# Attention scores over 256 keys in place of 210, 146 and 82

## The chip, the core and the metric

The kernel runs on one core of a Trainium2 chip. Its time is the device time of one execution in microseconds (us). The engines are named as in the profile: PE (TensorE's products), PEld (its weight loads), DVE (VectorE), ACT (ScalarE), POOL (GpSimd) and SP (SyncE, which issues most transfers). A line such as L606 is a line of the kernel before; the program of the changed kernel counts one line more from L467 on and two more from L598 on.

## The reference

One block of a streaming encoder on 1024 frames and 16 meta tokens, 1024 features wide: a SwiGLU half step, a mixer, a second half step, and RMS norms. The mixer adds a sliding-window attention and a gated linear attention, each behind a gate. The attention, cut to what matters here:

```python
CHUNK = 64; N_META = 16; ATT_HEADS = 8; ATT_KV_HEADS = 2; ATT_HEAD_DIM = 64
WINDOW = 128; WINDOW_CHUNKS = WINDOW // CHUNK
...
s_band = jnp.einsum('bcqkgd,bcskd->bkgcqs', qf, kb) * scale
s_band = s_band - slopes[None, :, :, None, None, None] * dist[None, None, None]
s_band = jnp.where(valid, s_band, -jnp.inf)
s_meta = jnp.einsum('bcqkgd,bmkd->bkgcqm', qf, km) * scale
p = jax.nn.softmax(jnp.concatenate([s_meta, s_band, s_sink], axis=-1), axis=-1)
of = (einsum(p[meta], vm) + einsum(p[band], vb))
```

So each chunk of 64 queries sees its own 64 keys, the 128 before them, the 16 meta keys and one learned sink per head. All of it is in 32-bit floating point.

## The kernel before

Features lie on partitions, tokens along the free dimension. To keep 32-bit precision, both operands of a product are split in two halves of type fp32r, and a product is three (L88 to L90): high by high, high by low, low by high. Weights are streamed in tiles of 128x1024 and split by ACT (L196, the high half) and DVE (L197, the low half).

The mixer goes through the keys' and values' projections, those of the queries, the attention, its branch matrix, the gated linear attention, the second branch and the output matrix. The attention loop runs over 16 chunks of 64 queries, c = 0 to 15.

Keys lie in `kh` (high halves, one tile for each of the two groups of heads) and `kl` (low halves), in 8 blocks of 146 columns: 16 meta keys, a column for the sink, a pad, and 128 frames (two chunks). A chunk's keys are one stretch of columns from `off`, `w` wide: 82 columns for c = 0, 146 for c = 1, and 210 for the other 14, which start either behind a block's meta keys or in the middle of its frames. `qs` holds the queries of a group: their high halves on the 64 partitions of the group's own head dimension, their low halves on the other 64.

`scores(c)` makes four products of a pair of halves, two for each group of heads: L606 takes all 128 rows of the queries against `kh`, which holds the high halves of the keys twice, and L607 the 64 rows of the high halves against `kl`. A bank of PSUM (512 columns) holds the two results of a group, 256 columns each. L610 adds the bias on DVE and takes the maximum of each row, L613 scales it, L615 is the exponential on ACT, L616 the reciprocal of the sums and L618 the normalisation, in four instructions, one for each pair of heads.

`turn` transposes the probabilities (L633, PE), by two kinds of key block (82, 128 or, for the second chunk, 18 keys), and splits them (L93 on ACT, L94 on DVE). `attend` multiplies them with the values (L649): eight products of 256 columns, or four for the first chunk, which has one kind of block. L655 to L660 put the result in the queries' place. `values` turns two chunks of values every second iteration (L566 to L570 on PE, L579 and L580 on ACT, L581 on DVE).

In each iteration of the loop, one unit of another projection stands between scores and attend: the fill, 24 products of 512 columns of the attention's gate (tile `pj`), which DVE evacuates at L455 (tile `g`) before it is stored.

```python
    for c in range(16):
        nxt = None
        turn(cur)
        if c < 15:
            nxt = scores(c + 1)
        if c % 2 == 0 and c < 14:
            values(c // 2 + 1)
        if fill:
            fill.pop(0)()
        attend(cur)
        cur = nxt
```

A scheduler of the language puts the instructions of each engine in an order of its own, by costs that it reckons for them. An engine works through its order as it stands, and waits at an instruction whose input is not there.

Of the kernel before, what the change touches and what calls it, by code (L numbers as in the profile page):

```python
# [29 lines left out]
# columns of w_in  # L30
# [5 lines left out]
def hybrid_kernel(  # L36
# [32 lines left out]
    def load_vectors(vs, eng):  # L69
        """per-feature vectors, transposed to one column per tile of 128 features"""  # L70
        at, n = vs[0][0], sum(v[2] for v in vs)
        vrow = ttile("vrow")[0:32, 0:P]
        for a, v, k in vs:
            eng.dma_start(out=vrow[a - at:a - at + k, :], in_=v.rearrange("o (k p) -> (o k) p", p=P))

        def turn():
            vps = bank("vps")
            nc.tensor.transpose(vps[:, 0:n], vrow[0:n, :], ident[0:n, 0:n])
            nc.scalar.copy(vec[:, at:at + n], vps[:, 0:n])
        return turn  # L80

    def mm(ps, wh, wl, xh, xl, between=()):
        """ps = sum_k w[k].T @ x[k] with both operands split in two exact halves."""
        n = len(wh)
        for k in range(n):
            if k < len(between):
                between[k]()
            nc.tensor.matmul(ps, wh[k], xh[k], start=(k == 0), stop=False)  # L88
            nc.tensor.matmul(ps, wh[k], xl[k], start=False, stop=False)  # L89
            nc.tensor.matmul(ps, wl[k], xh[k], start=False, stop=(k == n - 1))  # L90
# [5 lines left out]
    # ------------------------------------------------------------------ rms norms  # L96
# [3 lines left out]
    class Norm:  # L100
        """Splits g*h into two halves as h is completed, tile by tile, and gathers the squares for
        the row scales 1/rms, which the consumers apply to their products."""
# [14 lines left out]
        def put(self, m, c0, n, h, copy=None):  # L117
            """h: [P, n], final"""
            g = vec[:, self.g + m:self.g + m + 1]
            hi, lo = self.hi[m][:, c0:c0 + n], self.lo[m][:, c0:c0 + n]  # L120
            nc.scalar.activation(hi, h, AF.Copy, scale=g)
            if copy is not None and m % 2:
                nc.scalar.copy(copy, h)
            nc.vector.scalar_tensor_tensor(lo, h, g, hi.bitcast(F32), op0=ALU.mult, op1=ALU.subtract)  # L124
            if copy is not None and m % 2 == 0:
                nc.vector.tensor_copy(copy, h)
# [10 lines left out]
        def total(self, c0, n):  # L137
            """sums of squares, one token to a partition"""
            ps = bank("tot")
            for t, w in tiles_of(c0, n):  # L140
                nc.tensor.matmul(ps[0:w, t:t + 1], self.acc[:, t * P:t * P + w], ones[:, 0:1], start=True, stop=True)
            self.root(c0, n, ps)

        def root(self, c0, n, tot):
            """tot: sums of squares, one token to a partition"""
            ts = tiles_of(c0, n)
            for lo, hi, w in ((ts[0][0], min(ts[-1][0] + 1, 8), P), (8, ts[-1][0] + 1, NM)):
                if lo < hi:
                    r = self.tot[0:w, lo:hi]
                    nc.scalar.activation(r, tot[0:w, lo:hi], AF.Sqrt, bias=eps_t[0:w, :], scale=1.0 / D)  # L150
                    nc.vector.reciprocal(r, r)

        def widen(self, c0, n, dg):
            """1/rms by token to rows of 128"""
            ts = tiles_of(c0, n)
            for w in (P, NM):
                mine = [t for t, v in ts if v == w]
                if mine:
                    a, k = mine[0] * P - c0, len(mine)
                    nc.vector.tensor_copy(  # L160
                        dg[0:w, a:a + k * P].rearrange("p (a b) -> p a b", b=P),
                        self.tot[0:w, mine[0]:mine[0] + k].unsqueeze(2).to_broadcast([w, k, P]))

        def spread(self, c0, n, dg=None):
            """acc becomes 1/rms on all partitions"""
            ps = bank("rep")
            if dg is None:
                dg = ttile("dg")
                self.widen(c0, n, dg)
            for t, w in tiles_of(c0, n):  # L170
                a = t * P - c0
                nc.tensor.transpose(ps[:, a:a + w], dg[0:w, a:a + P], ident[0:w, 0:w])
            nc.scalar.copy(self.acc[:, c0:c0 + n], ps[:, 0:n])  # L173

    # ------------------------------------------------------------------ weights
    class Weights:
        """streams weights in tiles of 4 KiB a partition, splitting each in its two halves"""
# [4 lines left out]
        def raw(self, views, eng=None):  # L182
            """views: (rows of the tile, columns of the tile, source)"""
            pool = self.rs[self.j % len(self.rs)]
            self.j += 1
            raw = atile("raw")[:, 0:1024] if pool is act else pool.tile([P, 1024], F32, tag="raw", name="raw")
            for rows, dst, src in views:
                (eng or nc.sync).dma_start(out=dst(raw[rows, :]), in_=src)
            return raw
# [22 lines left out]
    # ------------------------------------------------------------------ swiglu, macaron half step  # L212
    class Ffn:
# [13 lines left out]
        def gate_up(self, f, hook=None, pump=None):  # L227
            """hook: called between products; says how many chunks have their row scales"""
# [59 lines left out]
    # ------------------------------------------------------------------ load, transpose, ffn 1  # L288
# [20 lines left out]
    def warm(n):  # L309
        """products that keep the clock of the tensor engine up while it waits for input"""  # L310
# [29 lines left out]
    def pump1(i):  # L340
        """the next chunk's transposes, between the products of this one"""
# [36 lines left out]
    # the first chunk tile by tile as it comes in  # L378
# [31 lines left out]
    # ------------------------------------------------------------------ mixer  # L410
# [3 lines left out]
    def after_products():  # L414
        """work that waited for products to cover its latency"""
# [11 lines left out]
    def project_units(views, chunks, evac, m=P, k=KT, pre=None):  # L427
        """closures, one per chunk of tokens: [m features] of u @ w_in"""
# [32 lines left out]
    # ---- attention: keys and values of each pair of chunks lie as [meta, sink, pad | 128 frames]  # L461
# [4 lines left out]
    W = 3 * 64 + MB  # L466
    qs = [ap_.tile([P, 16, 256], F32R, name=f"qs{g}") for g in range(2)]  # L467
# [16 lines left out]
    def build_bias():  # L484
        """-8 slope |distance| by parity of the chunk, group of heads and pair of heads in it"""
# [75 lines left out]
    def values(j):  # L561
        """values by token: the pair, [meta | first chunk], [second chunk | next meta], each as
        [high 0 | low 0 | low 1 | high 1 | high 0 | 0 | high 1] by group"""
# [22 lines left out]
    def scores(c):  # L586
        """probabilities of chunk c's queries, rows (pair of heads' halves, 64 queries)"""
# [8 lines left out]
        s.w, s.c = w, c  # L596
        mx = sml.tile([P, 4], F32, tag="mx", name="mx")
        sm = sml.tile([P, 4], F32, tag="sm", name="sm")  # L598
        s.p = ap_.tile([P, 4, W], F32, tag="p", name="p", bufs=2)
        for g in range(2):  # L600
            own = slice(g * 64, g * 64 + 64)
            ps = bank("sp")
            for a in range(2):
                q = qs[g][:, c, a * P:(a + 1) * P]
                o = ps[:, a * 256:a * 256 + w]
                nc.tensor.matmul(o, q, kh[g][:, off:off + w], start=True, stop=False)  # L606
                nc.tensor.matmul(o, q[own], kl[own, off:off + w], start=False, stop=True)  # L607
            for a in range(2):
                ga = 2 * g + a
                nc.vector.tensor_tensor_reduce(  # L610
                    s.p[:, ga, 0:w], ps[:, a * 256:a * 256 + w], bias[:, par * 4 + ga, W - w:W], 1.0, -3.0e38,
# [9 lines left out]
    def turn(s):  # L621
        """transposes the probabilities by kind of key block, and splits them"""
# [16 lines left out]
    def attend(s):  # L639
        """rows (group, head dim), columns (head of the group, query); takes the queries' place"""  # L640
# [9 lines left out]
        # a group's rows hold high V P, the other group's rows hold its low V high P  # L650
# [30 lines left out]
    # ---- attention's branch  # L681
    class Frames:
        """columns by frame of a view by chunk and place in it"""
# [7 lines left out]
    def branch(views, y, m0, load, evac, k=4):  # L691
        """two tiles of 128 columns of a [512, 1024] branch matrix"""
# [26 lines left out]
    # ---- gated linear attention, two chunks of 64 at a time  # L719
# [7 lines left out]
    # rows of gate_w, twice for the two halves of its input's weights: [high | high | low]  # L727
# [26 lines left out]
    def ev_tok(tok, meta):  # L754
        """scales and turns a tile of 128 features to rows of tokens"""
# [17 lines left out]
    # the forget gate's low-rank input, its two halves of weights side by side  # L773
# [21 lines left out]
    class Gla:  # L795
        """two heads"""
# [13 lines left out]
        def decays(self):  # L810
# [8 lines left out]
            # 16 log_a = min(z, 0) - log(1 + exp(-|z|)), summed up within each pair of chunks  # L819
# [4 lines left out]
            # against a pair's start, middle and end  # L824
# [116 lines left out]
    # ---- merge  # L941
# [37 lines left out]
    # ------------------------------------------------------------------ ffn 2 and the last norm  # L979
# [19 lines left out]
    def tail(t, last):  # L999
        """the last norm of 128 tokens, and their store"""  # L1000
# [63 lines left out]
```

## Time and profile before

| | |
|---|---|
| median of 3 runs | 2207.11 us (2205.82 to 2207.81) |
| span of the profiled execution, first to last instruction | 2204.7 us |
| mean granted clock of PE | 0.999 |
| DVE busy, over the span | 1020.6 us (46%) |
| attention loop, first score product to its last attend | 832.6 to about 1000 us |
| transfers, mean over the span | 67 GB/s |

No time other than its span is given for the profiled execution. Matmuls are pipelined: the duration of one row overlaps that of the next, so what a product takes of PE is read from the distance between two starts. A row of PEld is the load of the weights of a product; in a steady stream it starts with the product ahead of the one it is for.

### The profile page before, as it was taken

The page shows a single profiled execution, that of the slowest core. Times are in us where ns is not written, and L with a number is a line of the kernel's source. Part 1 is how long each engine was busy: PE and PEld are TensorE (multiplying, and loading weights), DVE is VectorE, ACT ScalarE, POOL GpSimd, SP SyncE. Part 2 cuts the span into 40 slices and gives each one's busy share as a digit, 9 for nine tenths or more (in the row PEclk, how much of TensorE's full clock was granted, in tenths as well). Part 3 has the DMA queues.
Part 4 walks back from the last instruction along what each step waited for, and adds up shares of the span by engine and source line. Part 5 has one row for each costly group of instructions (what it writes and reads, how often), then busy time and mean ns, then how long its engine had stood idle before and what let it go on. Part 6 is the DMA issues. An engine that isn't in the chain of part 4 may idle for free. (4 is left out here: it accounts for less than half of the span.)

```text
span 2204.7 us, 28132 instructions
## 1 busy us (share of the span) xinstructions
PE 2193.7 (100%) x11633; PEld 1942.1 (88%) x11633; DVE 1020.6 (46%) x1781; ACT 582.6 (26%) x1068; POOL 110.6 (5%) x157
## 2 busy tenths in 40 slices
PE   9999999999999999999999999999999999999998
PEld 8999999999999997888997788888888888888888
DVE  4544544445443546663524347334444444444434
ACT  6221111211111435553323233331111111111112
POOL 1000000000000350000100000210000000000003
PEclk9999999999999999999999999999999999999999
DMA  4211111111111221116211216541111101111102
GB/s 155 67 58 39 48 49 39 58 39 58 39 39 49 90 54 44 58 53 189 58 44 63 72 56 203 164 161 48 58 48 39 57 30 57 58 48 42 55 29 77
DMA packets 178192, 148.34 MB, mean 67 GB/s; under 512 B 15494, under 2 KB 151808, under 8 KB 178064
## 3 DMA queue, kind: packets, MB, share of 16 engines
q1 hardware_dynamic: 176400, 143.81, 21.3%
q10 hardware_dynamic: 1312, 2.63, 0.3%
q8 instruction: 91, 1.49, 0.3%
q14 instruction: 37, 0.30, 0.0%
q0 software_dynamic: 352, 0.11, 0.0%
HBM read 121.36 MB, written 25.17 MB: 66 GB/s over the span
## 5 line engine op out<-in xcount | busy, mean ns | idle before, releaser
L196 ACT CAST whi<-raw 128x1024 fp32r<-128x1024 f32 x182 | 188.9, 1049 | 661.2 <-PE pd L89 370.1
L88 PE MATMUL pd<-mh,whi 128*128 128x384 f32 (+3 forms) x912 | 313.7, 344 | 0.0
L89 PE MATMUL pd<-ml,whi 128*128 128x384 f32 (+3 forms) x912 | 313.6, 344 | 0.0
L90 PE MATMUL pd<-mh,wlo 128*128 128x384 f32 (+3 forms) x912 | 313.4, 344 | 0.0
L197 DVE TENSOR_TENSOR wlo<-raw,whi 128x1024 fp32r<-128x1024 f32 x179 | 218.2, 1233 | 54.0 <-ACT whi L196 48.8
L88 PE MATMUL pj<-u2h,whi 128*128 128x512 f32 (+2 forms) x608 | 230.3, 379 | 0.0
L90 PE MATMUL pj<-u2h,wlo 128*128 128x512 f32 (+2 forms) x608 | 225.8, 371 | 0.0
L89 PE MATMUL pj<-u2l,whi 128*128 128x512 f32 (+2 forms) x608 | 225.0, 370 | 0.0
L90 PEld LDWEIGHTS pd<-mh,wlo 128*128 128x128 f32 x912 | 171.7, 188 | 14.0
L89 PEld LDWEIGHTS pd<-ml,whi 128*128 128x128 f32 x912 | 171.5, 188 | 14.1
L88 PEld LDWEIGHTS pd<-mh,whi 128*128 128x128 f32 x912 | 171.6, 188 | 14.0
L88 PE MATMUL pu<-u1h,whi 128*128 128x384 f32 (+1 forms) x528 | 171.0, 324 | 0.6 <-ACT u1q L173 0.6
L88 PE MATMUL pg<-u1h,whi 128*128 128x384 f32 (+1 forms) x528 | 169.7, 321 | 1.7 <-ACT whi L196 1.7
L89 PE MATMUL pg<-u1l,whi 128*128 128x384 f32 (+1 forms) x528 | 169.9, 322 | 0.2 <-DVE u1l L124 0.2
L244 DVE TENSOR_TENSOR a<-pu,a 128x384 f32<-128x384 f32 (+2 forms) x110 | 64.7, 588 | 225.8 <-PE pu L90 225.4
L90 PE MATMUL pg<-u1h,wlo 128*128 128x384 f32 (+1 forms) x528 | 168.5, 319 | 0.6 <-DVE wlo L197 0.6
L89 PE MATMUL pu<-u1l,whi 128*128 128x384 f32 (+1 forms) x528 | 169.2, 320 | 0.0
L90 PE MATMUL pu<-u1h,wlo 128*128 128x384 f32 (+1 forms) x528 | 168.5, 319 | 0.4 <-POOL wlo L197 0.4
L276 DVE SCALAR_TENSOR_TENSOR g<-pd,g 128x512 f32<-128x512 f32 (+1 forms) x168 | 111.9, 666 | 118.0 <-PE pd L90 117.1
L276 DVE SCALAR_TENSOR_TENSOR h<-pd,h 128x384 f32<-128x384 f32 (+1 forms) x240 | 122.8, 518 | 80.1 <-PE pd L90 79.4
L242 ACT ACTIVATE a<-a 128x384 f32<-128x384 f32 (+2 forms) x110 | 60.3, 548 | 293.9 <-DVE a L241 293.7
L88 PE MATMUL pg<-u3h,whi 128*128 128x512 f32 x352 | 137.9, 392 | 0.0
(272 smaller groups left out, 3842.2 us busy)
## 6 DMA issues: line engine op xcount, KB each, us to landing
raw<-in_ffn_w_gate SPq DMA_DIRECT2D x44, 512.0 KB, 5.0
raw<-in_ffn_w_up SPq DMA_DIRECT2D x44, 512.0 KB, 4.0
raw<-in_ffn_w_down SPq DMA_DIRECT2D x44, 512.0 KB, 3.5
raw<-in_w_in SPq DMA_DIRECT2D x30, 512.0 KB, 3.9
gates<-g SPq DMA_DIRECT2D x32, 256.0 KB, 2.0
gl<-gates SPq DMA_DIRECT2D x32, 256.0 KB, 4.2
x<-in_x SPq DMA_DIRECT2D x8, 512.0 KB, 6.6
ga<-gates SPq DMA_DIRECT2D x16, 256.0 KB, 3.5
```

The lines of the kernel that those rows point to most:

```text
L88: nc.tensor.matmul(ps, wh[k], xh[k], start=(k == 0), stop=False)
L89: nc.tensor.matmul(ps, wh[k], xl[k], start=False, stop=False)
L90: nc.tensor.matmul(ps, wl[k], xh[k], start=False, stop=(k == n - 1))
L196: nc.scalar.copy(hi[:, 0:cols], raw[:, 0:cols])
L197: (eng or nc.vector).tensor_sub(lo[:, 0:cols], raw[:, 0:cols], hi[:, 0:cols].bitcast(F32))
L242: nc.scalar.activation(a, a, AF.Silu)
L244: nc.vector.tensor_mul(a, pu[:, 0:n], a)
L276: nc.vector.scalar_tensor_tensor(hm, ps[:, 0:n], 0.5, hm, op0=ALU.mult, op1=ALU.add)
```

## The change

The score products take 256 columns of keys for every chunk. They start at `k0`, which is `off`, or, where 256 columns from there would end beyond the keys (only for c = 15, by 46 columns), the last place at which they don't. The columns that a chunk doesn't attend to are computed and not read: L610 reads the `w` columns at `off - k0` of each result.

```diff
+    SW = 256
...
         s.w, s.c = w, c
+        k0 = min(off, 8 * KB - SW)
...
             for a in range(2):
                 q = qs[g][:, c, a * P:(a + 1) * P]
-                o = ps[:, a * 256:a * 256 + w]
-                nc.tensor.matmul(o, q, kh[g][:, off:off + w], start=True, stop=False)
-                nc.tensor.matmul(o, q[own], kl[own, off:off + w], start=False, stop=True)
+                o = ps[:, a * SW:(a + 1) * SW]
+                nc.tensor.matmul(o, q, kh[g][:, k0:k0 + SW], start=True, stop=False)
+                nc.tensor.matmul(o, q[own], kl[own, k0:k0 + SW], start=False, stop=True)
             for a in range(2):
                 ga = 2 * g + a
                 nc.vector.tensor_tensor_reduce(
-                    s.p[:, ga, 0:w], ps[:, a * 256:a * 256 + w], bias[:, par * 4 + ga, W - w:W], 1.0, -3.0e38,
+                    s.p[:, ga, 0:w], ps[:, a * SW + off - k0:a * SW + off - k0 + w], bias[:, par * 4 + ga, W - w:W], 1.0, -3.0e38,
                     op0=ALU.add, op1=ALU.max, accum_out=mx[:, ga:ga + 1])
```

The rest of the diff takes out comments and docstrings. The order that the scheduler makes changes as well, on PE, DVE and ACT, within the attention loop.

On DVE, iteration c = 4 before (L581 splits the values, L455 evacuates the fill, L659 begins with the attention's result):

```order
L613 TENSOR_SCALAR mx<-mx 128x4
L616 RECIPROCAL sm<-sm 128x4
L618 TENSOR_SCALAR p<-p,sm 128x210 x4
L581 TENSOR_TENSOR vz_6819<-vt,vz_6819 82x2x128
L455 TENSOR_TENSOR g<-pj,u2q 128x512
L659 TENSOR_TENSOR u<-po,qs_6813 64x256 x2
```

The same place of the changed kernel:

```order
L615 TENSOR_SCALAR mx<-mx 128x4
L455 TENSOR_TENSOR g<-pj,u2q 128x512
L618 RECIPROCAL sm<-sm 128x4
L582 TENSOR_TENSOR vz_6819<-vt,vz_6819 82x2x128
L620 TENSOR_SCALAR p<-p,sm 128x210 x4
L661 TENSOR_TENSOR u<-po,qs_6813 64x256 x2
```

The evacuation of the fill has moved ahead of the reciprocal and the normalisation, and the split of the values ahead of the normalisation. So it is for c = 0, 4, 8 and 12. For c = 2, 6, 10 and 14 the evacuation stands between the reciprocal and the normalisation; for odd c it stays behind the normalisation.

On PE, the transposes of the probabilities in iteration c = 4 and the first score products after them, before:

```order
L649 MATMUL po<-ptl,vz_6821 128x256
L633 MATMUL tp<-ident,p 82x128 x4
L633 MATMUL tp<-ident,p 128x128 x4
L606 MATMUL sp<-kh_6815,qs_6813 128x210
L607 MATMUL sp<-kl,qs_6813 128x210
```

And now:

```order
L651 MATMUL po<-ptl,vz_6821 128x256
L635 MATMUL tp<-ident,p 82x128
L635 MATMUL tp<-ident,p 128x128
L635 MATMUL tp<-ident,p 82x128
L635 MATMUL tp<-ident,p 128x128
L635 MATMUL tp<-ident,p 82x128
L635 MATMUL tp<-ident,p 128x128
L635 MATMUL tp<-ident,p 82x128
L635 MATMUL tp<-ident,p 128x128
L608 MATMUL sp<-kh_6815,qs_6813 128x256
L609 MATMUL sp<-kl,qs_6813 128x256
```

The transposes of the two kinds of block now alternate, pair of heads by pair of heads; the score products have 256 columns and stand in the same order, 128 rows and 64 rows in turn.

## The prediction

> **What bounds the kernel now.** I read the page's first two parts, then the busy time by stretch for the attention loop, then the groups by shape, and last the instructions in order of time.
>
> ```profile
> PE 2193.7 (100%) x11633; PEld 1942.1 (88%) x11633; DVE 1020.6 (46%) x1781; ACT 582.6 (26%) x1068; POOL 110.6 (5%) x157
> ...
> PEclk9999999999999999999999999999999999999999
> ```
>
> ```profile
> 845.00:1000.00 155.00, 155.00 (x775) 124.81 (x774) 100.95 (x327) 85.17 (x251) 0.00 (x0) 1.00 0.20 62
> ```
>
> The second fence is the stretch that holds most of the attention loop: its length, then the busy time of PE, PEld, DVE, ACT and POOL, then the clock. PE works in all of its 155 us, at full clock. So a microsecond that PE saves or waits there is a microsecond of the span, and DVE, ACT and the queues count only where PE comes to wait for them.
>
> The change touches the score products. These are their groups by shape, for L607; L606 has as many of each.
>
> ```profile
> L607 PE MATMUL sp<-kl,qs 64*128 64x210 f32 x56 | 20.2, 361 | 0.0
> ...
> L607 PE MATMUL sp<-kl,qs 64*128 64x146 f32 x4 | 1.3, 333 | 0.0
> ...
> L607 PE MATMUL sp<-kl,qs 64*128 64x82 f32 x4 | 1.2, 303 | 0.0
> ```
>
> So there are 112 products of 210 columns, 8 of 146 and 8 of 82. The 361 ns is a latency that overlaps the next product; what PE pays is the distance between two starts, read from the order of time:
>
> ```profile
> 855.31 0.34 PE L606 MATMUL sp<-kh,qs 128*128 128x210 f32 x1
> 855.58 0.36 PE L607 MATMUL sp<-kl,qs 64*128 64x210 f32 x1
> ...
> 857.34 0.36 PE L607 MATMUL sp<-kl,qs 64*128 64x210 f32 x1
> 857.63 0.50 PE L88 MATMUL pj<-u2h,whi 128*128 128x512 f32 x1
> ```
>
> Eight products of one chunk take 857.63 - 855.31 = 2.32 us, 0.29 each. Here is the start of the loop, with 82 columns, and PEld's rows (weight loads) between them:
>
> ```profile
> 834.76 0.40 PE L90 MATMUL pj<-u2h,wlo 128*128 128x512 f32 x1
> 834.77 0.19 PEld L606 LDWEIGHTS sp<-kh,qs 128*128 128x128 f32 x1
> ...
> 835.00 0.20 PE L606 MATMUL sp<-kh,qs 128*128 128x82 f32 x1
> 835.13 0.18 PEld L607 LDWEIGHTS sp<-kl,qs 64*128 64x128 f32 x1 [0.17 <-issue]
> 835.13 0.30 PE L607 MATMUL sp<-kl,qs 64*128 64x82 f32 x1
> ...
> 835.36 0.19 PEld L88 LDWEIGHTS pj<-u2h,whi 128*128 128x128 f32 x1
> 835.36 0.50 PE L88 MATMUL pj<-u2h,whi 128*128 128x512 f32 x1
> ```
>
> A product of 82 columns between two others of its kind costs 0.23 (835.13 to 835.36). From 82 to 210 columns it grows by 0.06 us, 0.47 ns a column, close to the 0.23 us for 512 columns of a fill product (834.76 to 835.00, 0.45 ns a column). So the short products do not stream more slowly. They carry a fixed 0.19 us (0.29 less 210 x 0.47 ns), as long as one weight load (0.18).
>
> **Where the 0.19 comes from** decides everything. The load of L606 starts at 834.77, one product ahead of its use, and is hidden. The load of L607 (64 rows) starts at 835.13 with its own product, and so does that of L88 (128 rows) after it. Two causes fit: the number of rows changes (128, 64, 128), or the product ahead is too short to hide a load. The trace has products of 256 columns whose rows change as well: the second chunk's value products, where 18 keys stand beside 128.
>
> ```profile
> 863.03 0.40 PE L90 MATMUL pj<-u2h,wlo 128*128 128x512 f32 x1
> ...
> 863.36 0.18 PEld L649 LDWEIGHTS po<-pth,vz 18*128 18x128 f32 x1 [0.36 <-issue]
> 863.36 0.38 PE L649 MATMUL po<-pth,vz 18*128 18x256 f32 x1
> 863.47 0.18 PEld L649 LDWEIGHTS po<-ptl,vz 18*128 18x128 f32 x1
> ...
> 863.58 0.27 PE L649 MATMUL po<-ptl,vz 18*128 18x256 f32 x1
> 863.78 0.19 PEld L649 LDWEIGHTS po<-pth,vz 128*128 128x128 f32 x1
> 863.78 0.39 PE L649 MATMUL po<-pth,vz 128*128 128x256 f32 x1
> ...
> 864.01 0.28 PE L649 MATMUL po<-ptl,vz 128*128 128x256 f32 x1
> ```
>
> With 256 columns, and even behind one of 512, the load still waits at each change of rows (863.36 and 863.78 start with their product), and is ahead where rows stay (863.47 for 863.58). A product of this shape without a change costs 0.12 (eight of them below, 893.74 to 894.70). The change costs 0.08 in the distance ahead (863.58 to 863.78 is 0.20) and 0.11 in the one behind (863.78 to 864.01 is 0.23): together the same 0.19. I take the change of rows as the cause.
>
> ```profile
> 1043.98 0.40 PE L90 MATMUL br<-qs,wlo 128*128 128x512 f32 x1
> 1044.21 0.34 PE L783 MATMUL pj<-u2h,w 128*32 128x384 f32 x1
> ```
>
> The Trainium skill, "TensorEngine Tiling", section "Key Properties", states that changing the tiling mode, not merely the tile, drains TensorE. By that rule each L606/L607 pair pays its two changes at any number of columns, and the products get 3.2 us dearer; without it they could get 21.0 us cheaper. The 18-row products above agree with it (0.19 a change), while weights of 32 columns in place of 128 cost nothing (1043.98 to 1044.21 is the ordinary 0.23), so here it holds for rows alone.
>
> **The change, part by part.** *The products.* Their number, order of rows and loads stay; only columns are added. One of 256 columns costs 0.19 + 256 x 0.47 ns = 0.31, and 0.12 + 0.08 + 0.11 = 0.31 by the 18-row rows. By the same line 146 columns cost 0.26 now. So 112 x (0.31 - 0.29) + 8 x (0.31 - 0.26) + 8 x (0.31 - 0.23) = 2.2 + 0.4 + 0.6 = **+3.2 us**, all on PE. No row shows 64 rows with 256 columns. The low end is the 0.12 of full rows: the 128 products take 36.4 us now (112 x 0.29 + 8 x 0.26 + 8 x 0.23) and would take 15.4, -21.0. The high end adds 0.10 and 0.11 (863.03 to 863.36 is 0.10 over 0.23): 0.33 each, +5.8. I take 0.31, the nearest rows.
>
> *The order on DVE.* The gate's evacuation L455 is moved ahead of the normalisation (L618 before, L620 after) in the eight iterations c = 0, 2, ... 14. In c = 0, 4, 8, 12 it also passes the reciprocal, and L581 passes the normalisation. L455 waits for the fill's last product, and behind it in DVE's queue now stand the probabilities for which the transposes L633 wait; DVE takes its instructions in order. These are the rows of c = 4, and two of c = 3 for the delay from the fill to L455:
>
> ```profile
> 883.51 0.40 PE L90 MATMUL pj<-u2h,wlo 128*128 128x512 f32 x1
> ...
> 883.94 0.69 DVE L455 TENSOR_TENSOR g<-pj,u2q 128x512 f32<-128x512 f32 x1
> ```
>
> ```profile
> 892.58 0.18 DVE L616 RECIPROCAL sm<-sm 128x4 f32<-128x4 f32 x1 [2.18 <-ACT p L615]
> ...
> 892.79 1.05 DVE L618 TENSOR_SCALAR p<-p,sm 128x210 f32<-128x210 f32 x4
> ...
> 893.51 0.40 PE L90 MATMUL pj<-u2h,wlo 128*128 128x512 f32 x1
> ...
> 893.74 0.28 PE L649 MATMUL po<-pth,vz 128*128 128x256 f32 x1
> ...
> 893.76 0.42 DVE L581 TENSOR_TENSOR vz<-vt,vz 82x256 fp32r<-82x256 f32 x1
> ...
> 894.09 0.68 DVE L455 TENSOR_TENSOR g<-pj,u2q 128x512 f32<-128x512 f32 x1
> ...
> 894.60 0.90 PEld L633 LDWEIGHTS tp<-ident,p 128*82 128x82 f32 x8
> 894.70 1.04 PE L633 MATMUL tp<-ident,p 128*82 128x128 f32 x8
> ...
> 895.49 0.34 PE L606 MATMUL sp<-kh,qs 128*128 128x210 f32 x1
> ```
>
> Before, the probabilities are done at 892.79 + 1.05 = 893.84, while the fill still runs, 0.76 ahead of the first transpose's load (894.60). After, with the same fill: it ends at 893.91, L455 runs from 893.94 to 894.62 (as in c = 3, 0.03 behind the fill). The next may start about 0.08 before that ends (as L455 at 894.09 does within L581). Then the reciprocal, 0.10 until L581 may start, 0.34 until the normalisation starts: 894.98, and it ends 1.05 later at 896.03. The last pair of transposes waits for its end, 0.05 for the signal and 0.10 for its load (894.60 to 894.70), so starts at 896.18 and 896.29 (eight take 895.49 - 894.70, 0.11 each, the last distance 0.03), and the next scores at 896.32 in place of 895.49: **0.83 us** in which PE has nothing else in its queue. In c = 2, 6, 10, 14 reciprocal and L581 do not stand between: 0.83 - 0.10 - 0.34 = 0.4. In c = 0 the attention's value products, which cover the wait, are 4 in place of 8 (0.48 less cover): 0.83 + 0.48 = 1.3. Sum 3 x 0.83 + 4 x 0.4 + 1.3 = **+5.4 us**. Between 4.2 (signal and load cost nothing, 8 x 0.15 less) and 6.5 (0.13 more each).
>
> *What costs nothing.* The bias addition L610 reads 210 columns as before, and its shift is not zero only for the last chunk (46 columns). It starts at DVE's own turn, after the split of the transposes, not at the last score product. The casts moved on ACT (L93 behind L579 and L580 in three iterations) end before the fill does, which DVE now waits for. If that cover fails, each costs at most the two casts. SP's and POOL's queues stand in the same order.
>
> Sum: 3.2 + 5.4 = +8.6. Against the profiled span of 2204.7 that gives 2213.3; the median of the runs, 2207.11, lies 2.4 above the span, which I leave as it is: **2215.7 us**, +0.39%. A measurement of this kernel can tell about 0.2% (4.4 us) from no change.
>
> **Rivals.** *Long products hide the loads (faster).* If what exposes the load is a short product and not the change of rows, 256 columns end it: -21.0. For it: L606's load behind 512 columns is hidden. Against it: the 18-row rows with the same 256 columns. PE would then come 8 x 0.17 = 1.4 us earlier to the transposes of each chunk. The 0.76 of slack above, and 0.33 until the fourth transpose needs the last probabilities, leave it some 0.35 short in the eight odd iterations (2.9) and about 0.1 more in the even ones (1), beside the 5.4. Together -21.0 + 5.4 + 2.9 + 1 = -11.7: 2195.4. It decides at 0.24 a product (36.4 - 5.4 over 128): below that the kernel is faster.
>
> *The new place of L455 costs PE nothing (same).* If the wait is covered after all, the columns alone remain: +3.2, 2210.3. For it: PE's loads run ahead of products where they can. Against it: the last transposes cannot load probabilities that DVE has not written, and nothing stands between them and the scores in PE's queue.
>
> **How the numbers follow.** Forecast 0.76, the first rival 0.13, the second 0.11. The forecast's own range is 2.2 + 4.2 to 5.8 + 6.5, that is 2213.5 to 2219.4. Down to 2210 it takes in the second rival, and only the first is left out: 2210 to 2219.5. Faster by over 0.2% is the first rival, 0.13; within 0.2% the second, 0.11; slower 0.76.
>
> **What would show it.** In the changed profile the score products have starts 0.31 apart, and the load of each starts with its own product. PE, without idle time in the loop now, waits eight times for the normalisation ahead of the transposes, 0.4 to 1.3 us each, 5.4 in all; DVE waits for the fill at L455 in these. Starts 0.12 apart would prove the first rival right, and idle PE without waits of L455 would make the second step wrong.

## The result, and the profile after

| | before | after |
|---|---|---|
| median of 6 runs each, taken side by side | 2206.98 us (2205.80 to 2207.81) | 2214.32 us (2214.09 to 2215.15) |
| span of the profiled execution | 2204.7 us | 2213.0 us |
| mean granted clock of PE | 0.999 | 0.999 |

The ratio is 1.0035 [1.0024, 1.0047]: the kernel is slower by 0.35%, 7.3 us, where the prediction had 0.39%. Line numbers of the changed kernel are 2 higher in the attention loop: the score products are L608 and L609, the normalisation L620, the transposes L635, the value products L651.

The page's first part of the changed kernel:

```profile
span 2213.0 us, 28131 instructions
...
PE 2198.2 (99%) x11633; PEld 1941.0 (88%) x11633; DVE 1020.3 (46%) x1781; ACT 582.8 (26%) x1068; POOL 110.6 (5%) x157
```

The same number of instructions on PE, and no longer 100% busy. The stretch that was full before, with the same columns (length, then busy time of PE, PEld, DVE, ACT, POOL, then the clock):

```profile
845.00:1000.00 155.00, 152.01 (x734) 118.23 (x733) 96.70 (x317) 80.71 (x243) 0.00 (x0) 1.00 0.19 55
```

PE now idles 3.0 of 155 us, and starts 734 products in place of 775: it idles, and the products cost more. The idle time understates the loss, since a product's row lasts longer than the distance to the next start (0.38 for 0.31 in the rows of L609 below). What a wait costs has to be read from starts as well. The groups by shape:

```profile
L609 PE MATMUL sp<-kl,qs 64*128 64x256 f32 x64 | 24.4, 380 | 0.0
L608 PE MATMUL sp<-kh,qs 128*128 128x256 f32 x64 | 24.1, 376 | 0.0
```

All 128 score products have one shape now. And this is c = 4, in order of time:

```profile
897.17 0.40 PE L90 MATMUL pj<-u2h,wlo 128*128 128x512 f32 x1
...
897.60 0.69 DVE L455 TENSOR_TENSOR g<-pj,u2q 128x512 f32<-128x512 f32 x1 [2.46 <-PE pj L90]
...
898.21 0.17 DVE L618 RECIPROCAL sm<-sm 128x4 f32<-128x4 f32 x1
...
898.29 0.39 DVE L582 TENSOR_TENSOR vz<-vt,vz 82x256 fp32r<-82x256 f32 x1
...
898.60 1.03 DVE L620 TENSOR_SCALAR p<-p,sm 128x210 f32<-128x210 f32 x4
899.04 0.83 PEld L635 LDWEIGHTS tp<-ident,p 128*82 128x82 f32 x8 [0.74 <-PE po L651]
899.07 1.04 PE L635 MATMUL tp<-ident,p 128*82 128x128 f32 x8 [0.57 <-DVE p L620]
...
899.87 0.36 PE L608 MATMUL sp<-kh,qs 128*128 128x256 f32 x1
900.16 0.18 PEld L609 LDWEIGHTS sp<-kl,qs 64*128 64x128 f32 x1
900.16 0.38 PE L609 MATMUL sp<-kl,qs 64*128 64x256 f32 x1
...
900.47 0.39 PE L608 MATMUL sp<-kh,qs 128*128 128x256 f32 x1
```

DVE stands at L455 for 2.46 us until the fill's last product is through; then come the reciprocal, the values' split and the normalisation, one after the other, and PE waits for the last of them, the normalisation. From the fill's last start to the first score product it is 899.87 - 897.17 = 2.70 us; before it was 1.98 (893.51 to 895.49). Behind that, the load of L609 starts with its own product (900.16 twice), and the products stand 0.31 apart (900.16 to 900.47). The waits from 845 to 1010 us, most of the loop:

```profile
DVE g L455 <- PE pj L90: 24.7, 16, 3.3
...
PE tp L635 <- DVE p L620: 3.0, 7, 0.9
...
PEld tp L635 <- DVE p L620: 1.4, 2, 1.1
```

The columns are the sum, the number of times, and the longest. Before, the first of these rows read 2.4 us in one time, and the other two weren't there. Of the 24.7 us, 16.3 are in the even iterations; the rest stands in the odd ones, where PE waits for none of it.

Where the 8.3 us between the two spans came from, by distances of starts. The eight products of a chunk take 2.48 us: +0.16 in each of 14 chunks, +0.38 where there were 146 columns, +0.62 where there were 82 (each product by its own distance, since fill products stand between those). That is 3.3. From the fill's last product to the next product after the transposes:

| c | 0 | 2 | 4 | 6 | 8 | 10 | 12 | 14 | sum |
|---|---|---|---|---|---|---|---|---|---|
| before, us | 1.51 | 1.97 | 1.99 | 1.97 | 1.97 | 1.98 | 1.97 | 1.97 | |
| after, us | 2.65 | 2.31 | 2.70 | 2.31 | 2.70 | 2.31 | 2.57 | 2.30 | |
| more | 1.14 | 0.34 | 0.72 | 0.34 | 0.74 | 0.33 | 0.60 | 0.33 | 4.5 |

For odd c the distances agree to 0.01. So 3.3 + 4.5 = 7.8 us, which is all that the time from the first score product to the end of the loop grew by. The other 0.55 of the 8.3 lies ahead of the loop: the first score product starts at 833.14 in place of 832.59, and the products ahead of it are late by as much from the first 71 us on, where nothing was changed. The medians differ by 7.3.

### The profile page after: what moved, and what is told of

Its sections match the earlier page's. It is cut to its first block, busy times and chain, and to the rows that moved or that the text cites. A ratio compares the mean times of both kernels' runs of the same rounds, so it can differ in the third digit from the quotient of the medians.

```text
span 2213.0 us, 28131 instructions
## 1 busy us (share of the span) xinstructions
PE 2198.2 (99%) x11633; PEld 1941.0 (88%) x11633; DVE 1020.3 (46%) x1781; ACT 582.8 (26%) x1068; POOL 110.6 (5%) x157
## 3 DMA queue, kind: packets, MB, share of 16 engines
q10 hardware_dynamic: 1312, 2.63, 0.3%
## 5 line engine op out<-in xcount | busy, mean ns | idle before, releaser
L89 PE MATMUL pg<-u3l,whi 128*128 128x512 f32 x352 | 137.7, 391 | 0.0
```

## The experiments

Two things were to be tested: that the score products' fixed cost is the change of rows and not their shortness, and that the evacuation's place costs 4 to 5 us by itself.

**1. No change of rows, 210 columns.** The kernel before, with the second product over all 128 rows:

```diff
-                nc.tensor.matmul(o, q[own], kl[own, off:off + w], start=False, stop=True)
+                nc.tensor.matmul(o, q, kl[:, off:off + w], start=False, stop=True)
```

> The kernel before with one edit: the second score product takes all 128 rows of the queries against all 128 rows of the low halves of the keys, in place of the 64 rows of its group. It thereby also adds the low halves of the queries times the low halves of the other group's keys. Columns stay 82, 146 and 210, the order of all engines stays. Theory (the change between 128 and 64 rows exposes a weight load of 0.19 us): no product changes rows, so starts of products of 210 columns come about 0.11 us apart in place of 0.29, each load starts one product ahead, and the 128 products take about 14 us in place of 36.4. PE then comes 1.4 us earlier to each chunk's transposes, and with 1.1 us of slack there waits some 0.35 us for the probabilities in each of 16 iterations: -22 + 5.5, a time near 2190 us (2185 to 2196). Rival (a product of fewer than 256 columns cannot hide the next load): starts stay 0.29 apart and the time stays at 2207 within 1 us.

Measured: 2189.42 us (2188.89 to 2190.02), ratio 0.9921 [0.9907, 0.9936], so 17 us faster than before. In order of time (L605 and L606 are the two score products here):

```profile
933.26 0.27 PE L606 MATMUL sp<-kl,qs 128*128 128x210 f32 x1
933.27 0.19 PEld L605 LDWEIGHTS sp<-kh,qs 128*128 128x128 f32 x1
933.37 0.27 PE L605 MATMUL sp<-kh,qs 128*128 128x210 f32 x1
933.38 0.19 PEld L606 LDWEIGHTS sp<-kl,qs 128*128 128x128 f32 x1
933.48 0.27 PE L606 MATMUL sp<-kl,qs 128*128 128x210 f32 x1
```

Each load starts one product ahead of its own, and the products stand 0.11 apart with the same 210 columns: short products hide their loads. The first rival of the prediction, by which 210 columns are too few, has fallen here. PE waits a little for the normalisation in the even iterations now (2.32 to 2.48 us from the fill's last product to the scores, in place of 1.97, and for c = 0 2.46 in place of 1.51), since it comes to the transposes earlier; in the odd ones, where the theory had waits too, it is 1.99 as before, but for c = 3 (2.05).

**2. The same in the changed kernel, 256 columns.** The edit is the same.

> The changed kernel with the same edit: 256 columns and all 128 rows in the second score product. Theory: starts 0.12 us apart, 128 products in about 15.4 us; the order of DVE is that of the changed kernel, so PE waits for the normalisation in the eight even iterations by at least the 4.5 us of the changed kernel, and a little in the odd ones: about 2195 us (2190 to 2200), slower than the same edit with 210 columns by 4 to 8 us. Rival: 0.12 apart too, but then 5 us or more below the kernel with 210 columns and 128 rows, which stays at 0.29.

Measured: 2190.41 us (2189.78 to 2191.19), ratio 0.9927 [0.9910, 0.9944]; the products stand 0.12 apart. It is 23.9 us faster than the changed kernel, and only 1.0 slower than the run of 210 columns, where 4 to 8 were expected. The miss has a reason: in the run of 210 columns the even iterations wait as well, for the same normalisation (2.32 to 2.48 us there, 2.35 to 2.70 here), so the evacuation's place finds little left to cost.

**3. Half the changes, in two ways, and a quarter.** If a change of rows has a price, fewer of them must cost less in proportion. First across two banks, in the order 128, 128, 64, 64 (g is the group, a the half of it):

```diff
+        pss = [bank("sp") for g in range(2)]
+        for a in range(2):
+            os = [ps[:, a * 256:a * 256 + w] for ps in pss]
+            for g in range(2):
+                nc.tensor.matmul(os[g], qs[g][:, c, a * P:(a + 1) * P], kh[g][:, off:off + w], start=True, stop=False)
+            for g in range(2):
+                own = slice(g * 64, g * 64 + 64)
+                nc.tensor.matmul(os[g], qs[g][own, c, a * P:(a + 1) * P], kl[own, off:off + w], start=False, stop=True)
         for g in range(2):
-            own = slice(g * 64, g * 64 + 64)
-            ps = bank("sp")
...
+            ps = pss[g]
```

> The kernel before (210, 146 and 82 columns), with the same 128 score products per kind in another order: of the eight of a chunk the four over 128 rows and the four over 64 rows stand in pairs (128, 128, 64, 64, 128, 128, 64, 64) across the two groups' banks, so that there are 4 changes of the row count for a chunk in place of 8. The order of VectorE's work is that of before. Theory (each change of rows costs about 0.18 us, one that is missing costs nothing): 16 chunks x 4 changes fewer x 0.18 = 11.5 us less on TensorE, about 2195.5 (2193 to 2199); the products' starts alternate between about 0.11 and 0.29 apart. Rival (what the run over all 128 rows saved came from the operands or from the doubled rows of the second product, and not from the number of changes): 2207, no change. Second rival (a product into the same bank as its forerunner is what waits): 2207 or a full 17 less, 2190, as every product now follows one into another bank.

Measured: 2193.21 us (2192.54 to 2194.03), ratio 0.9940 [0.9927, 0.9954]: 13.5 us less, where the theory had 11.5 (2193 to 2199) and the rivals 0 or 17. The rows say where the other 2 come from:

```profile
953.98 0.48 PE L604 MATMUL sp<-kh,qs 128*128 128x210 f32 x2
954.38 0.19 PEld L607 LDWEIGHTS sp<-kl,qs 64*128 64x128 f32 x2
954.38 0.36 PE L607 MATMUL sp<-kl,qs 64*128 64x210 f32 x2
...
954.68 0.33 PE L566 MATMUL vt<-ident,vcat 128*128 128x128 f32 x1
```

Two products over 64 rows take 0.36 together, which is what one took before, and their two loads 0.19, which is what one takes. They start 0.003 to 0.004 us apart: one uses rows 0 to 63, the other rows 64 to 127, and they run side by side. So this run saves four changes and a product's time twice in each chunk; the eight products take 1.38 us. The starts are 0.20 or 0.003 apart, and 0.29 behind a pair over 64 rows, not 0.11 and 0.29 by turns as the theory had it.

The next run keeps one bank and one set of rows, so that nothing runs side by side (128, 64, 64, 128):

```diff
                 o = ps[:, a * 256:a * 256 + w]
-                nc.tensor.matmul(o, q, kh[g][:, off:off + w], start=True, stop=False)
-                nc.tensor.matmul(o, q[own], kl[own, off:off + w], start=False, stop=True)
+                if a == 0:
+                    nc.tensor.matmul(o, q, kh[g][:, off:off + w], start=True, stop=False)
+                nc.tensor.matmul(o, q[own], kl[own, off:off + w], start=(a == 1), stop=(a == 0))
+                if a == 1:
+                    nc.tensor.matmul(o, q, kh[g][:, off:off + w], start=False, stop=True)
```

> The kernel before (210, 146 and 82 columns), one bank for a group as before; of the second half of each group the product over 64 rows stands ahead of the one over 128 rows (128, 64, 64, 128), so that the two products over 64 rows, which use the same 64 rows, follow each other and so do those over 128: 4 changes of the row count for a chunk in place of 8, the same products and columns. VectorE's order is that of before. Theory (a change costs 0.18 us, nothing else matters): the eight products of a chunk take 8 x 0.11 + 4 x 0.18 = 1.60 us in place of 2.32, 16 x 4 x 0.18 = 11.5 us in all, 2206.7 - 11.5 = 2195.2 (2194 to 2197). The run with two banks saved 13.5 since its products over rows 0 to 63 and 64 to 127 started 0.003 us apart, side by side; here both use the same rows, and start 0.11 apart. Rival (the saving of the two-bank run comes from the second bank): 2206.7, no change.

Measured: 2196.94 us (2196.32 to 2197.53), ratio 0.9957 [0.9941, 0.9974], 9.6 us less where the theory had 11.5, and inside its range. In order of time (L607 and L610 have 128 rows, L608 has 64):

```profile
957.50 0.28 PE L607 MATMUL sp<-kh,qs 128*128 128x210 f32 x1
957.70 0.29 PEld L608 LDWEIGHTS sp<-kl,qs 64*128 64x128 f32 x2
957.71 0.47 PE L608 MATMUL sp<-kl,qs 64*128 64x210 f32 x2
958.11 0.19 PEld L610 LDWEIGHTS sp<-kh,qs 128*128 128x128 f32 x1
958.11 0.37 PE L610 MATMUL sp<-kh,qs 128*128 128x210 f32 x1
```

Two products on the same 64 rows take 0.47, and from the first of them to the product behind is 0.40, where side by side it was 0.30 (954.38 to 954.68). Starts are 0.20 apart throughout (957.50 to 957.71, and 0.40 for the two that follow). The load at a change starts with its own product; the two loads of a pair take 0.29 together, 0.18 and 0.19 each, so the second starts about 0.11 behind the first. Eight products take 1.68 us, four changes dearer than the 0.96 of the first run: 0.18 a change, and 0.16 by what was saved within the eight (2.32 - 1.68 over four).

With the second half in reverse across two banks (128, 128, 64, 64, 64, 64, 128, 128) two changes a chunk remain. Its core:

```diff
+            high = lambda g: nc.tensor.matmul(pss[g][:, a * 256:a * 256 + w], qs[g][:, c, a * P:(a + 1) * P], kh[g][:, off:off + w], start=(a == 0), stop=(a == 1))
+            low = lambda g: nc.tensor.matmul(pss[g][:, a * 256:a * 256 + w], qs[g][g * 64:g * 64 + 64, c, a * P:(a + 1) * P], kl[g * 64:g * 64 + 64, off:off + w], start=(a == 1), stop=(a == 0))
+            for f in (high, low) if a == 0 else (low, high):
+                f(0)
+                f(1)
```

> As the run with two banks, and the second half in reverse: 128, 128, 64, 64, 64, 64, 128, 128 over the two groups' banks, with rows 0 to 63 and 64 to 127 in turn; 2 changes of the row count for a chunk, and the products over 64 rows side by side in pairs. It computes exactly the products of before (another order of the sums). Theory: the eight products take 6 x 0.11 + 2 x 0.18 = 1.02 us in place of 2.32, which is 20.8 us on TensorE; given back are waits for the normalisation in the even iterations, as in the run over all 128 rows (0.96 us for eight products, 17.3 saved in all, 0.4 us of wait in each of seven iterations): 2206.7 - 17 = 2189.7 (2188.5 to 2191.5). Rival (no wait comes): 2186. Second rival (the products side by side aren't faster than one after the other when four stand in a row, 0.11 each): 2193.

Measured: 2190.19 us (2189.98 to 2191.40), ratio 0.9927 [0.9912, 0.9942], as the theory has it. Eight products take 1.10 us (expected 1.02), and the wait for the normalisation is there again: 2.16 to 2.42 us from the fill to the scores in the even iterations. With the two runs before it this gives the price of a change; only the order of the same products differs in all three. Take 0.12 for a product and count two side by side as one: then it is (1.10 - 6 x 0.12) / 2 = 0.19 a change here. In the two-bank run and in the kernel before, the last change stands behind the eight products, and the product that follows them takes 0.07 more on average than in the one-bank run: (1.38 + 0.07 - 6 x 0.12) / 4 = 0.18 and (2.32 + 0.07 - 8 x 0.12) / 8 = 0.18, as in the one-bank run.

**4. The evacuation's place alone.** A first try wrote VectorE's order out by hand as the program text has it, in the kernel before as a control and in the changed one:

```diff
+    with tc.manual_schedule(engines={nc.vector.engine}):
-    for c in range(16):
-        nxt = None
+        for c in range(16):
+            nxt = None
...
```

> The kernel before, with DVE held to the order in which the attention loop is written: the evacuation of the fill stands behind the normalisation in every iteration. It is the control for the next run. Theory: no wait of PE in the loop is made or removed, 2207 us within 2 us.

> The changed kernel, 256 columns, with DVE held to the written order as in the control, so that the evacuation of the fill is never ahead of the normalisation. Theory (waits of 4.5 us come from the place of the evacuation in DVE's queue, 3.5 us from the columns): the waits of PE ahead of the transposes go, starts of score products stay 0.31 apart, and the time is 3.5 us above the control, about 2210.5 us. Rival (the waits come from the transposes of the two kinds of block alternating, or from the longer products themselves): it stays within 1.5 us of the changed kernel's 2214.3.

Measured: 2263.49 us for the control, ratio 1.0260 [1.0245, 1.0276], and 2286.28 for the changed kernel, 1.0362 [1.0346, 1.0377]. The control should have been 2207 and missed by 56, so neither tells anything of the change. The control's waits from 845 to 1010 us show where the order hurts:

```profile
ACT p L615 <- DVE mx L613: 75.2, 12, 11.8
DVE g L455 <- PE pj L90: 48.5, 6, 8.3
...
PE tp L633 <- DVE p L618: 20.4, 11, 3.1
```

DVE stands at L455 for up to 8.3 us at a time, and from the fill's last product to the scores it takes 2.98 to 5.57 us in most iterations, where it was 1.97 to 1.99.

The second try forces one order of two instructions and leaves the rest to the scheduler. In the changed kernel, a copy of one column from the normalised probabilities into the tile of the evacuation makes the evacuation stay behind:

```diff
             g = ttile("g")
+            if hold:
+                nc.vector.tensor_copy(g[:, 0:1], hold.pop().p[:, 3, 0:1])
             nc.vector.tensor_mul(g[:, 0:n], ps[:, 0:n], r)
...
             nxt = scores(c + 1)
+            hold[:] = [nxt]
```

> The changed kernel (256 columns) with one more copy of 128x1 elements on VectorE in each fill's evacuation, from the next chunk's normalised probabilities into the tile that the evacuation then overwrites: the evacuation can't be put ahead of the normalisation, in any iteration. Results are the same. Theory (the changed kernel's slowdown has two parts, wider products 3.3 us and the evacuation's place 4 to 4.5 us): the waits of TensorE for the normalisation in the even iterations go, 2214.3 - 4.3 = 2210.0 (2209 to 2211.5). Rival (the place of the evacuation costs nothing on the whole, what is lost there is taken from slack elsewhere): 2214.3, no change against the changed kernel. Second rival (the evacuation that now comes later is itself waited for): over 2214.3.

Measured: 2210.00 us (2209.45 to 2211.01, 11 runs), ratio 1.0017 [1.0008, 1.0025]. That is 4.3 less than the changed kernel, or 4.0 where each of the two is set against the kernel before as it ran beside it (2206.98 and 2206.67). c = 4 again:

```profile
894.73 1.05 DVE L624 TENSOR_SCALAR p<-p,sm 128x210 f32<-128x210 f32 x4
895.15 0.40 PE L90 MATMUL pj<-u2h,wlo 128*128 128x512 f32 x1
...
896.27 0.69 DVE L459 TENSOR_TENSOR g<-pj,u2q 128x512 f32<-128x512 f32 x1
...
897.12 0.36 PE L612 MATMUL sp<-kh,qs 128*128 128x256 f32 x1
```

The normalisation runs beside the fill, and the scores come 1.97 us after the fill's last start, as before. The score products are still 0.31 apart. So the columns alone cost 3.3 us (2210.00 - 2206.67), and the place 4.0 to 4.3. The transposes of the two kinds of block alternate in c = 4 of this run too, 0.11 apart as before, so their alternation, the rival of the first try, is not what cost time.

The opposite, in the kernel before with its 210 columns: the evacuation forced ahead in the even iterations, by an instruction that adds zero times the evacuated tile to the reciprocals:

```diff
             nc.vector.tensor_mul(g[:, 0:n], ps[:, 0:n], r)
+            hold[:] = [g]
...
             nc.vector.reciprocal(sm, sm)
+            if hold and s.c % 2:
+                nc.vector.scalar_tensor_tensor(sm, hold[0][:, 0:4], 0.0, sm, op0=ALU.mult, op1=ALU.add)
```

The reciprocal and the normalisation are also called behind the fill in these iterations.

> The kernel before (210, 146 and 82 columns) with the evacuation of the fill forced ahead of the normalisation in the even iterations, as it stands in the changed kernel: one more VectorE instruction of 128x4 elements adds 0 times the evacuated tile to the reciprocals (results stay the same). Theory (the place of the evacuation alone costs 4 to 4.5 us): 2207.0 + 4.3 = 2211.3 (2210 to 2213), with gaps of 0.3 to 1.1 us in TensorE ahead of the scores of the odd chunks; with the run where the changed kernel has it behind, the two parts add up to the whole. Rival (it costs nothing at 210 columns): 2207. Score products stay 0.29 apart.

Measured: 2212.29 us (2211.78 to 2214.94), ratio 1.0027 [1.0017, 1.0037], +5.6 where +4.3 was expected. c = 4:

```profile
895.42 0.40 PE L90 MATMUL pj<-u2h,wlo 128*128 128x512 f32 x1
895.85 0.69 DVE L457 TENSOR_TENSOR g<-pj,u2q 128x512 f32<-128x512 f32 x1 [0.69 <-PE pj L90]
896.58 0.16 DVE L623 SCALAR_TENSOR_TENSOR sm<-g,sm 128x4 f32<-128x4 f32 x1
896.78 1.05 DVE L625 TENSOR_SCALAR p<-p,sm 128x210 f32<-128x210 f32 x4
...
898.05 0.34 PE L609 MATMUL sp<-kh,qs 128*128 128x210 f32 x1
```

2.63 us from the fill to the scores. The added instruction stands between the two in all eight iterations. It starts when the evacuation has ended and takes 0.20 until the normalisation may start, which is 0.93 behind the evacuation's start here (895.85 to 896.78). Each iteration loses 0.65 to 0.67, and the first 1.08: 5.7 in sum. In the changed kernel nothing stands between them for c = 2, 6, 10 and 14, where the normalisation starts 0.61 behind the evacuation's start, and those lose 0.34.

**5. Is there more to be had?** Both measures of the changed kernel together, all 128 rows and the evacuation behind:

> 256 columns, both score products over all 128 rows (the low keys' part of the other group is added too, which is of the size of a rounding), and the evacuation behind the normalisation in every iteration, as in the run before this one. Without the extra copy this kernel took 2190.4. Theory (the evacuation's place costs what it costs in the changed kernel, 4 us): 2186.5. Rival (with the score products 1.3 us shorter a chunk the normalisation comes late whichever stands first, as in the run of 210 columns over 128 rows, where it stands first and TensorE waits 0.3 to 0.5 us in the even iterations): 2189 to 2190.5, no gain.

Measured: 2192.19 us (2191.54 to 2192.97), ratio 0.9936 [0.9921, 0.9952]. It is the rival's answer, no gain, though it lies above the rival's range too: 1.8 lost against the run without the copy. PE waits in the odd iterations too (2.36 to 2.41 us from the fill to the scores for c = 3 to 11, in place of 1.99).

And the run of 210 columns over 128 rows, with the values' transposes written behind the fill:

```diff
-        if c % 2 == 0 and c < 14:
-            values(c // 2 + 1)
         if fill:
             fill.pop(0)()
+        if c % 2 == 0 and c < 14:
+            values(c // 2 + 1)
         attend(cur)
```

> The run of 210 columns over all 128 rows (2189.4), and the transposes and splits of the value keys written behind the fill in place of ahead of it, in the even iterations. With it VectorE does none of their subtractions between the score evacuations and the normalisation, and ScalarE none of their copies ahead of the exponentials. Theory (in that run TensorE waits 0.3 to 0.5 us in each of seven even iterations, since the normalisation comes late): the waits go, 2189.4 - 7 x 0.4 = 2186.6 (2186 to 2187.5). Rival (the fill's end sets it, or the value transposes now stand where something waits for them): 2189.4, no gain, or more.

Measured: 2198.34 us (2197.44 to 2198.69), ratio 0.9963 [0.9949, 0.9977], 8.9 us slower than without the edit: a miss. Its rows of an odd iteration, and of the score product that this normalisation depends on:

```profile
928.98 0.34 PE L605 MATMUL sp<-kh,qs 128*128 128x210 f32 x1
...
929.26 0.37 ACT L579 CAST vz<-vt 82x256 fp32r<-82x256 f32 x1 [1.57 <-DVE vz L581]
...
931.33 0.86 DVE L658 TENSOR_TENSOR u<-po,qs 64x256 f32<-64x256 f32 x2 [0.98 <-ACT t L655]
...
933.76 0.36 DVE L609 CUSTOM_DVE_ANT_0 p<-sp,bias 128x210 f32<-128x210 f32 x1
...
937.43 1.05 DVE L617 TENSOR_SCALAR p<-p,sm 128x210 f32<-128x210 f32 x4
937.88 1.16 PEld L632 LDWEIGHTS tp<-ident,p 128*128 128x128 f32 x8 [1.46 <-issue]
937.91 1.39 PE L632 MATMUL tp<-ident,p 128*128 128x128 f32 x8 [1.28 <-DVE p L617]
```

The wait of the even iterations went into the odd ones and grew. The values' casts on ACT and splits on DVE stand at the end of an even iteration now, ahead of the attention's result. ACT waits 1.57 us for a split before its next cast (929.26), comes late to the copies of the result, and DVE waits 0.98 us for those (931.33) ahead of its splits of the probabilities. So DVE comes to the next scores 4.8 us after the first of their products; from there the maxima, the exponentials and the normalisation take the rest. From the fill to the scores it is 3.2 to 3.8 us in the odd iterations, and 2.47 to 2.50 in the even ones from c = 2 on, though the three value transposes are now part of it. The loop has little slack on DVE and ACT once PE is 17 us faster. The lowest median of all kernels here is the first run's (2189.42); of those that compute exactly the products of before it is that of the one with two changes (2190.19). Their ratios' intervals overlap, so the two are not told apart.

## Why the prediction was right, point by point

*PE bounds the loop, so its cost is the span's.* Right: 3.3 and 4.5 us of PE's starts make 7.8 us, all that the span grew by from the first score product on.

*The fixed 0.19 us of a score product is the change of rows, and stays at 256 columns.* Right, and now shown: without changes the products stand 0.11 to 0.12 apart at 210 and at 256 columns alike, and with half the changes, on one bank, 9.6 of the 17 us come. The Trainium skill ("TensorEngine Tiling", "Key Properties"), by which a change of the tiling mode drains TensorE, agrees with these runs for a change between 128 and 64 rows. A change costs 0.18 to 0.19; where every product follows a change, that is the fixed part of each product that the prediction read as 0.19. But "change of rows" is too wide a name. The eight value products of c = 4, from which the prediction took its 0.12 without a change, go between 128 and 82 rows:

```profile
893.86 0.28 PE L649 MATMUL po<-ptl,vz 128*128 128x256 f32 x1
893.86 0.19 PEld L649 LDWEIGHTS po<-pth,vz 82*128 82x128 f32 x1
893.98 0.28 PE L649 MATMUL po<-pth,vz 82*128 82x256 f32 x1
```

The load over 82 rows starts one product ahead, and the distance is 0.12. So a change between 128 and 82 rows costs nothing here, and the price stands for 128 beside 64 and, by the prediction's rows, beside 18. Where between 64 and 82 it begins, no run shows.

*+3.2 us for the columns.* 3.3 by the run with the evacuation held behind, and 3.3 by the starts; the distance is 0.31, as forecast. The chunk of 82 columns grew by 0.62, where 0.6 was put in.

*+5.4 us for the evacuation's place.* The mechanism was right in all eight iterations, the size about 1 us too large: 4.5 by the starts, 4.0 to 4.3 by the run. In c = 4 the forecast had 0.83 and the trace has 0.72. L455 starts 0.43 behind the fill's last product in both. The steps on DVE then took a little less than put in (1.00 from L455 to the normalisation for 1.04, 1.03 for its length in place of 1.05), and the last transposes start about 0.10 behind the normalisation's end, for which 0.15 was put in (0.10 for a load, and 0.05 for a signal, for which no row was given). In c = 2, 6, 10, 14 it is 0.34 for 0.4, in c = 0 it is 1.14 for 1.3, and c = 12, counted with c = 4 and 8, lost only 0.60: the split of the values is shorter there (0.26 for 0.39), and the normalisation starts 0.87 behind L455 in place of 1.00.

*The sum.* The span was forecast at 2213.3 and is 2213.0. That it comes so close is in part luck: the loop grew by 7.8 where 8.6 was forecast, and 0.55 came ahead of the loop, where nothing was forecast. Of the 1.4 us that the median lies under the forecast, most is the step from span to median: 2.4 was carried over from before, 1.3 was found (2214.32 - 2213.0). In every execution for which both are known, the time lies 1.7 to 1.9 us above the span, so the profiled execution before was probably 0.7 us quicker than its median.

*The rivals.* The faster one is refuted by the run of 210 columns over full rows. Its price was of the right kind: without the changes of rows, the changed kernel runs at 2190.41, where 2195.4 had been worked out. Of the terms there, the 21.0 holds (19.4 in the score products, 1.2 in the products right behind them); the 5.4 is 4.5, and neither the 2.9 for the odd iterations (by its own figures 1.4 - 0.76 - 0.33 = 0.31 each, 2.5; the trace has 1.99 us from the fill to the scores, as before) nor the 1 more in the even ones (2.35 to 2.70, as without the edit) came: 2207.1 - 21.0 + 4.5 = 2190.6. The other, that L455's place costs nothing, had 2210.3, which is what the kernel takes where the place is undone (2210.0).

*What costs nothing.* The odd iterations agree to 0.01 us, and with the evacuation held behind the even ones agree to 0.02, so the bias addition and its shift cost PE nothing. The casts moved on ACT weren't tried alone.

## What to carry to other kernels

Before a size is rounded up or down to please an engine, look at what the fixed part of each instruction's distance is made of; here it was the alternation of 128 and 64 rows, and ordering the same products by row count, some of them side by side, is worth 16 us where the number of columns is worth 3. A change of sizes may also move a scheduler's order elsewhere, so compare the order of every engine that the bounding one waits for, and price each move by the wait that ends last. An order can be pinned for two instructions with a tiny dependent one, which tests it without upsetting the rest; rewriting the whole order by hand tested nothing.

## What the runs showed of the hardware

Products over rows 0 to 63 and over rows 64 to 127, in different banks, run side by side: they start 0.003 us apart, the product behind the two starts 0.30 us after them where it is 0.40 behind two on the same rows, and their loads go together as well (0.19 for both). A change between 128 and 64 rows costs 0.18 to 0.19 us with 210 columns, and leaves the starts 0.29 apart where every product changes and 0.20 apart where every second does. A change between 128 and 82 rows costs nothing (0.12 apart, with 256 columns).
